# Down products of a feed-forward by seven products of quarters, and three of four weight sums by accumulating transfers

## The chip, the cores and the metric

The kernel runs on one core of one Trainium2 chip. The time is device microseconds from start to end of one execution. The kernel before took 2272.09 us in the median of 3 runs (2272.01 to 2272.13). The engines are named as the profile names them: PE multiplies matrices (PEld is its weight load), DVE, ACT and POOL work on vectors, SP issues transfers. Each engine works through its own queue in order; an instruction that waits holds up everything behind it on that engine.

## The reference

Two groups of tokens, 512 of a new stream and 32 of a running one, go through two layers of width 1024 and share all weights. Each layer is: half a feed-forward, a mixer (a Mamba-2 scan in layer 0, stick-breaking attention in layer 1), half a feed-forward, and a gated per-layer embedding (called PLE below). So there are four feed-forwards, and each computes

```python
def swiglu(h, w_gate, w_up, w_down):
    return (jax.nn.silu(h @ w_gate) * (h @ w_up)) @ w_down
x = x + 0.5 * swiglu(rms_norm(x, g), w_gate, w_up, w_down)   # 1024 -> 2816 -> 1024
```

Everything is in 32 bit floats. Between the second feed-forward and the third, keys and values for the attention are made from x.

## The kernel before, in words

The 544 tokens are the columns of every tile (two halves of 272), model and hidden width lie on the partitions in blocks of 128. The hidden width 2816 is 22 row blocks, the model width 8 chunks `x[0]` to `x[7]`. A product of a 128 x 128 weight block with 128 x 272 columns takes three matmuls, because every operand is split in a high part (`whi`, `xh`, `hh`: a rounding copy, made by ACT or POOL) and a low part (`wlo`, `xl`, `hl`: the difference, made by DVE or POOL): high by high, high by low, low by high. So one block on all 544 columns is 6 matmuls of 272 columns.

Class `Sevens` runs one feed-forward. Row blocks 0 to 3 of the hidden width are done plainly ("p" units: gate or up weights of one block, 48 matmuls). The other 18 go in 9 pairs. For a pair, gate and up weights are cut into quarters, and seven products of sums of quarters with sums of activation quarters (tiles `xfh`, `xfl`, made once per feed-forward) stand for eight. The seven are named by their weight operand: a11, s3 = a11+a21, s2 = s3+a22, a12, s1 = a21+a22, a22, s4 = s2+a12; each is a step of 24 matmuls. The four sums are made by DVE (a few by POOL). The results are put together, scaled by the norm's factor `r`, and turned into the hidden block. The down product is plain in the kernel before: for a group of 4 or 6 row blocks, eight "d" units, one per chunk m, with all blocks of the group accumulated in one bank of PSUM, then one DVE instruction (`leave`) that adds half of it to `x[m]`. The last group's d units stand at the end of the feed-forward; each `x[m]` that leaves them is at once prepared for the next norm (`Norm.ops`: xh by ACT, xl by DVE, a square by ACT, its sum into `acc` by POOL).

The order of all this is set by `Plan`: chains of work are generators that ask for slots, events and engines, and the planner, with fixed costs per instruction, lets the chain go next that can start first; where several could, the one with the lower rank goes (preparing the next norm 2, `leave` 9, weights 10, PE 20). What comes out is a fixed order of instructions on PE, DVE, ACT and POOL. The weights of a step may be split only into a free buffer of three (`NW = 3`): the buffer of the step three places earlier, which is free when PE has ended that step. Raw weights come by SP's queue into slots of their own, one for each quarter (`a11`, `a21`, `a22`, `a12`), which are refilled when they are free.

Nearly every instruction is recorded by one helper, so the profile gives all of them one line (L194) and tiles tell them apart. In the profile's names `mm` is a PSUM bank, `gu` a hidden block in work, `a` and `s` are raw quarters and their sums.

Of the kernel before, what the change touches and what calls it, by code (L numbers as in the profile page):

```python
# [49 lines left out]
FIRST = [0, 1, 2, 3], [0, 1, 2, 3], [0, 1, 2, 3], [0, 1, 2, 3]  # L50
GROUPS = [(4, 5), (6, 7)], [(8, 9), (10, 11)], [(12, 13), (14, 15)], [(16, 17), (18, 19), (20, 21)]
AFTER, UNTIL = 3, 14

NH = 6
# [127 lines left out]
def _body(tc, io):  # L182
# [22 lines left out]
    with ExitStack() as ctx:  # L205
# [17 lines left out]
        x = [pool.tile([P, T], F32, tag=f"x{c}", name=f"x{c}") for c in range(KC)]  # L223
# [209 lines left out]
        def opening(norm, psum, tmp):  # L433
# [8 lines left out]
            more = tmp.tile([P, 2, 512], F32, tag="a12", name="a12")[:, :, :].rearrange("p j k -> p (j k)")  # L442
# [112 lines left out]
        class Sevens:  # L555

            NW = 3

            def __init__(self, plan, i, norm, bank, tmp, ring, roles, after, first=(), opened=None, ahead=None, done=None):
                self.plan, self.i, self.bank, self.tmp, self.ring = plan, i, bank, tmp, ring
                self.groups, self.after, self.opened, self.norm, self.ahead, self.done = (FIRST[i],) + GROUPS, after, opened, norm, ahead, done
# [4 lines left out]
                self.hs, self.loaded, self.raw, self.gu = {}, {}, {}, {}  # L570
                self.units, waiting = [], []
                for g, items in enumerate(self.groups):
                    steps = sum(isinstance(it, tuple) for it in items) * 7
                    step = sent = 0
                    for it in items:
                        if not isinstance(it, tuple):
                            self.units += [("p", it, j) for j in range(2)] if it or not opened else []
                            continue

                        for s in (0, 3, 1, 2, 4, 5, 6) if g == 0 or not any(isinstance(v, tuple) for v in self.groups[0]) and it == items[0] and g == 1 else range(7):  # L580
                            self.units.append(("s", it, s))
                            step += 1
                            while waiting and step >= AFTER and sent < (step - AFTER + 1) * KC / (UNTIL - AFTER):
                                self.units.append(waiting.pop(0))
                                sent += 1
                    self.units += waiting
                    waiting = [("d", g, m) for m in range(KC)]
                self.units += waiting
                self.last_step = max(k for k, u in enumerate(self.units) if u[0] == "s")
# [4 lines left out]
            def members(self, g):  # L594
                return [f for it in self.groups[g] for f in (it if isinstance(it, tuple) else (it,))]


            def fetch_plain(self):
                i = self.i
                for k, u in enumerate(self.units):  # L600
# [7 lines left out]
                    if u[0] == "p":  # L608
                        self.raw[k] = fetch_w(io["wgu"][i, u[1], u[2]], 1024)
                    elif u[0] == "w":  # L610
                        self.raw[k] = fetch_w(u[1], 1024)
                    else:
                        fs = self.members(u[1])
                        self.raw[k] = fetch_w(io["wd"][i, u[2], :, fs[0] * P:(fs[-1] + 1) * P], len(fs) * P)
                    yield "spawn", self.arrive(("raw", k), 1.0 if k < 3 else 4.5)

            def fetch_quarter(self, name):
                r, c = int(name[1]) - 1, int(name[2]) - 1
                for items in self.groups:
                    for it in items:  # L620
                        if isinstance(it, tuple):
                            yield "get", name
                            t = self.raw[it, name] = self.tmp.tile([P, 2, 512], F32, tag=name, name=name)
                            nc.sync.dma_start(t, io["wgu"][self.i, it[r], :, :, c * 512:(c + 1) * 512].rearrange("j p k -> p j k"))
                            yield "spawn", self.arrive(("raw", it, name))
# [5 lines left out]
            def total(self, out, a, b):  # L631
                return either(self.plan, v_cost(1024), 2.4, lambda e: e.tensor_tensor(out=out, in0=a, in1=b, op=ALU.add))

            def weights(self):
                raw, tmp = self.raw, self.tmp
                for k, u in enumerate(self.units):
# [6 lines left out]
                    if u[0] != "s":  # L643
                        yield "wait", ("raw", k)
                        if u[0] == "d":
                            n = len(self.members(u[1])) * P
                        src, free = raw[k], "a12" if k == 0 and self.opened else "raw"
                    else:
                        it = u[1]
                        name = STEPS[u[2]][0]  # L650
                        if name[0] == "a":
                            yield "wait", ("raw", it, name)
                            src = raw[it, name]
                            if name == "a22":
                                free = "a22"
                        elif name == "s3":
                            yield "wait", ("raw", it, "a21")
                            yield "get", "s3"
                            src = raw[it, "s3"] = tmp.tile([P, 2, 512], F32, tag="s3", name="s3")
                            yield self.total(src, raw[it, "a11"], raw[it, "a21"])  # L660
                            yield "wait", ("part", self.index[it, 0])
                            yield "put", "a11"
                        elif name == "s2":
                            yield "wait", ("raw", it, "a22")
                            yield "get", "s2"
                            src = raw[it, "s2"] = tmp.tile([P, 2, 512], F32, tag="s2", name="s2")
                            yield self.total(src, raw[it, "s3"], raw[it, "a22"])
                            yield "spawn", self.release(("part", self.index[it, 1]), "s3")
                        elif name == "s1":
                            src = raw[it, "a21"]  # L670
                            free = "a21"
                            yield self.total(src, src, raw[it, "a22"])
                        else:
                            src = raw[it, "s2"]
                            free = "s2"
                            yield "wait", ("part", self.index[it, 2])
                            yield self.total(src, src, raw[it, "a12"])
                            yield "spawn", self.release(("part", self.index[it, 3]), "a12")
                        src = src[:, :, :].rearrange("p j k -> p (j k)")
# [11 lines left out]
                    yield "spawn", self.halve(k, n, src, hi, lo, free), -2 if k == 0 and self.opened else 10  # L691

# [12 lines left out]
            def dense(self):  # L705
                banks = {}
                for k, u in enumerate(self.units):
# [3 lines left out]
                    if u[0] == "s":  # L711
                        it, s = u[1], u[2]
                        name, place, slot = STEPS[s]
                        if s == 0:
                            A, B, D, X = self.roles
                            at = {"A": A, "B": B, "D": D}
                            self.roles = [B, A, D, X]
# [5 lines left out]
                        if s == 2:  # L723
                            yield "wait", ("c0", it)
                        elif s == 4:
                            yield "wait", ("c1", it)
                        elif s == 5:
                            yield "wait", ("c3", it)
                        elif s == 6:
                            yield "wait", ("c2", it)  # L730
                        yield "wait", ("part", k)
                        for c in range(4):
                            if isinstance(slot, int):
                                yield "wait", ("xf", c, slot)
                            yield "T", 0.753, lambda: self.step(ps, self.loaded[k], c, slot, s in (0, 1, 3) and c == 0, s in (3, 5, 6) and c == 3)
                        yield "put", "w"
                        if s in (0, 1, 2, 4):
                            yield "spawn", self.save(it, ps, {0: 0, 1: 3, 2: 1, 4: 2}[s]), 20
# [30 lines left out]
                    else:  # L769
                        g, m = u[1], u[2]  # L770
                        fs = self.members(g)
                        final = g == len(self.groups) - 1
                        b = self.roles[(0, 3, 2, 1)[(k - self.last_step - 1) % 4] if k > self.last_step else 3]
                        yield "wait", ("part", k)
                        yield "get", f"b{b}"
                        ps = banks[g, m] = self.bank(b)

                        early = len(fs) - 2 if final and m < 2 else len(fs)
                        order = [(k, ps, e) for e in range(early)]
                        if final and m == 1:  # L780
# [10 lines left out]
                        if m == KC - 1:  # L791
                            for _ in fs:
                                yield "put", "h"
# [1371 lines left out]
```

## Time and profile before

| | before |
|---|---|
| median of 3 runs | 2272.09 us |
| the profiled execution, first to last instruction | 2270.6 us |
| PE busy | 2245.7 us, 17937 matmuls |
| DVE, ACT, POOL busy | 1675.8, 1008.2, 575.8 us |
| granted TensorE clock, mean | 0.997 |
| HBM read | 204.83 MB, mean 93 GB/s with the writes |

Busy times can overlap on one engine: an instruction's record ends after the next has begun. The distance from one start to the next tells what an instruction costs in a dense stretch. The four feed-forwards lie at about 0 to 372, 810 to 1175, 1262 to 1633 and 1800 to 2171 us of the execution; the mixers lie between the first and second and between the third and fourth.

### The profile page before, as it was taken

To read this page: it belongs to the slowest core of one execution; us is meant where nothing else is said; L and a number is where in the kernel's file an instruction comes from. 1 tells how busy PE (TensorE), PEld (TensorE's weight loads), DVE (VectorE), ACT (ScalarE), POOL (GpSimd) and SP (SyncE) were. 2 spreads that over 40 slices of the span, in tenths; PEclk is the share of its full clock that TensorE was granted. 3 is DMA by queue.
4 is the path that set the end of the run, shared out by engine and by line. 5 is a ranking of instruction groups with operands and counts; after the bars stand their busy time and mean duration, and the time that the engine had idled before them with its cause. 6 is when DMAs were issued, how large, how long until landed. Compare 5 with 4: busy or idle time off the path is not lost.

```text
span 2270.6 us, 42781 instructions
## 1 busy us (share of the span) xinstructions
PE 2245.7 (99%) x17937; PEld 2200.5 (97%) x17937; DVE 1675.8 (74%) x2195; ACT 1008.2 (44%) x1478; POOL 575.8 (25%) x546
## 2 busy tenths in 40 slices
PE   9999999999999999999999999999999999999997
PEld 9999999999899999999999999999997999999997
DVE  7777786778877676777857767778689676777857
ACT  5333334567756453333345533333568343333353
POOL 1222222254323122221221121212244222222214
PEclk9999999999999999999999999999999999999998
DMA  5233323333333232333232423332311233233232
GB/s 169 85 96 105 97 66 89 113 110 96 114 101 96 86 119 85 93 107 95 65 108 85 132 80 107 93 104 69 88 49 52 61 112 99 83 108 94 68 101 77
DMA packets 111537, 213.18 MB, mean 94 GB/s; under 512 B 12401, under 2 KB 33521, under 8 KB 111345
## 3 DMA queue, kind: packets, MB, share of 16 engines
q1 hardware_dynamic: 108464, 204.92, 30.2%
q10 hardware_dynamic: 2880, 5.53, 0.7%
q8 instruction: 141, 2.31, 0.4%
q14 instruction: 52, 0.42, 0.1%
HBM read 204.83 MB, written 5.60 MB: 93 GB/s over the span
## 4 chain that ended last, share of the span: by engine, by line
PE 94%; DVE 3%; ACT 2%; issue 1%; DMA 1%; POOL 0%; SPq 0%; DVEq 0%; ACTq 0%; POOLq 0%
PE mm L194 83%; PE z L194 4%; PE aux L194 3%; PE f L194 1%; PE tr L194 1%; PE o L194 1%; DVE wlo L194 1%; ACT whi L194 1%; DVE x L194 0%; DVE fu L194 0%; DMA wraw<-in_wpg 0%; DVE xl L194 0%; DMA x<-in_x 0%; DVE rm L194 0%; DVE y L194 0%
## 5 line engine op out<-in xcount | busy, mean ns | idle before, releaser
L194 PE MATMUL mm<-xh,whi 128*128 128x272 f32 x2096 | 512.9, 293 | 2.0 <-ACT xh L194 0.6
L194 PE MATMUL mm<-xl,whi 128*128 128x272 f32 x2096 | 506.5, 289 | 0.3 <-DVE xl L194 0.3
L194 PE MATMUL mm<-xh,wlo 128*128 128x272 f32 x2096 | 504.9, 289 | 1.8 <-DVE wlo L194 1.8
L194 PEld LDWEIGHTS mm<-xh,whi 128*128 128x128 f32 x2096 | 356.9, 189 | 12.7 <-issue 9.2
L194 PEld LDWEIGHTS mm<-xh,wlo 128*128 128x128 f32 x2096 | 356.8, 189 | 2.2 <-DVE wlo L194 2.2
L194 PEld LDWEIGHTS mm<-xl,whi 128*128 128x128 f32 x2096 | 357.0, 189 | 0.5 <-DVE xl L194 0.5
L194 ACT ACTIVATE whi<-wraw 128x1024 fp32r<-128x1024 f32 (+3 forms) x217 | 186.3, 859 | 357.5 <-PE mm L194 258.3
L194 PE MATMUL mm<-xfh,whi 128*128 128x272 f32 x1152 | 332.4, 289 | 0.0
L194 PE MATMUL mm<-xfl,whi 128*128 128x272 f32 x1152 | 332.3, 288 | 0.0
L194 PE MATMUL mm<-xfh,wlo 128*128 128x272 f32 x1152 | 332.2, 288 | 0.0
L194 DVE TENSOR_TENSOR wlo<-wraw,whi 128x1024 fp32r<-128x1024 f32 (+3 forms) x252 | 255.7, 1015 | 69.5 <-ACT whi L194 53.1
L194 PE MATMUL mm<-hh,whi 128*128 128x272 f32 x1408 | 291.6, 288 | 0.0
L194 PE MATMUL mm<-hh,wlo 128*128 128x272 f32 x1408 | 291.2, 288 | 0.0
L194 PE MATMUL mm<-hl,whi 128*128 128x272 f32 x1408 | 291.0, 288 | 0.0
L194 ACT ACTIVATE whi<-a 128x1024 fp32r<-128x1024 f32 x127 | 134.8, 1062 | 320.4 <-PE mm L194 214.8
L194 DVE TENSOR_TENSOR wlo<-a,whi 128x1024 fp32r<-128x1024 f32 x145 | 178.0, 1227 | 102.2 <-ACT whi L194 67.7
L194 PEld LDWEIGHTS mm<-hl,whi 128*128 128x128 f32 x1408 | 221.4, 189 | 0.0
L194 PEld LDWEIGHTS mm<-hh,whi 128*128 128x128 f32 x1408 | 221.1, 188 | 0.0
L194 PEld LDWEIGHTS mm<-hh,wlo 128*128 128x128 f32 x1408 | 220.6, 189 | 0.0
L194 PEld LDWEIGHTS mm<-xfh,wlo 128*128 128x128 f32 x1152 | 217.1, 188 | 0.0
L194 PEld LDWEIGHTS mm<-xfl,whi 128*128 128x128 f32 x1152 | 217.1, 188 | 0.0
L194 PEld LDWEIGHTS mm<-xfh,whi 128*128 128x128 f32 x1152 | 217.0, 188 | 0.0
(296 smaller groups left out, 4077.6 us busy)
## 6 DMA issues: line engine op xcount, KB each, us to landing
a<-in_wgu SPq DMA_DIRECT2D x145, 512.0 KB, 3.9
wraw<-in_wd SPq DMA_DIRECT2D x128, 256.0 KB, 2.7
wraw<-in_win SPq DMA_DIRECT2D x41, 512.0 KB, 3.6
wraw<-in_wgu SPq DMA_DIRECT2D x29, 512.0 KB, 3.6
wraw<-in_wd SPq DMA_DIRECT2D x32, 384.0 KB, 3.2
ab<-acs_d SPq DMA_DIRECT2D x16, 512.0 KB, 4.6
wraw<-in_wout SPq DMA_DIRECT2D x16, 512.0 KB, 3.7
wraw<-in_wpg SPq DMA_DIRECT2D x16, 512.0 KB, 3.6
```

The source lines that it names most:

```text
L194: ins = getattr(self.engine, op)(*args, **kw)
```

## The change

The first 16 of the 18 paired row blocks now go through the down product by seven products of quarters too. Their hidden pairs are joined in groups of three, three and two (`UNITED`), and each group takes two units "h" (a = 0 and 1), each of seven steps; a step has 6 matmuls for each pair of the group, thus 18, 18 or 12. I write h(g,a), and x(p) for the gate and up steps of pair p. Step order in an h unit is a11, a12, s2, s3, s1, a22, s4. h(0,0) and h(0,1) follow x(3), h(1,0) and h(1,1) follow x(6), h(2,0) and h(2,1) follow x(8), the last. The other six row blocks stay plain: 0 to 3 in four units after x(0), 20 and 21 in two units at the very end (four chunks each, 12 matmuls a chunk).

The hidden activations need sums of quarters as well (`outcome`: four DVE instructions a pair, and seven quarters instead of four are split in high and low). A product of quarters is added straight to x from PSUM by DVE (`add`), up to the place where the bank is used on: the steps s2, s1 and s4 accumulate on top of a11's bank, and each may start only when the add of the step before on that bank has been done (the `saved` events).

Of the four weight sums, s3, s1 and, for gate and up, s4 are now made by transfers: a plain one of one quarter by SP, then an accumulating one of the other quarter, issued from POOL's queue (`added`, `fourth`). s2 stays on DVE or POOL, and so does s4 in the h units. Smaller parts: x lies in tiles of two chunks; raw weights in memory are laid out by quarter; and keys and values wait in DRAM between the two middle feed-forwards and come back by three transfers from POOL when the attention starts.

```diff
+NPLAIN = 4
+NPAIRS = 9
+UNITED = (0, 1, 2), (3, 4, 5), (6, 7)
...
+                for p in range(NPAIRS):
+                    self.loads.append(("x", p))
+                    self.units += [("s", ("x", p), s) for s in ((0, 3, 2, 1, 4, 5, 6) if p == 0 else range(7))]
+                    if p == 0:
+                        self.units += [("d", 0, q) for q in range(4)]
+                    for g, ps in enumerate(UNITED):
+                        if p == ps[-1] + 1:
+                            self.loads += [("h", g, a) for a in range(2)]
+                            self.units += [("s", ("h", g, a), s) for a in range(2) for s in (0, 3, 2, 1, 4, 5, 6)]
+                self.units += [("d", 1, q) for q in range(2)]
...
+            def added(self, key, tag, name):
+                yield "sleep", 4.5
+                yield "D", 1.0, lambda: G.dma_start(self.raw[key, tag][:, :self.width(key)], self.quarter_of(key, name), accum_op=ALU.add)
+                yield "sleep", 5.0
+                yield "set", ("raw", key, tag)
...
+            def fourth(self, it):
+                yield "wait", ("part", self.index[it, 2])
+                yield "D", 1.0, lambda: G.dma_start(self.raw[it, "s2"], self.quarter_of(it, "12"), accum_op=ALU.add)
+                yield "sleep", 5.0
+                yield "set", ("raw", it, "s4")
...
+                        if s in (2, 4, 5, 6):
+                            yield "wait", ("saved", it, {2: 0, 4: 2, 5: 1, 6: 4}[s])
                         yield "wait", ("part", k)
...
+            def add(self, it, s, ps, slot):
+
+                row, col = {0: (0, 0), 1: (1, 1), 2: (1, 0), 3: (0, 0), 4: (1, 1), 5: (1, 0), 6: (0, 1)}[s]
+                to = x2[2 * row + it[2]][:, :, col * H:(col + 1) * H]
+                yield "W", v_cost(T) + 0.06, lambda: V.scalar_tensor_tensor(out=to, in0=ps[:, :, :H], scalar=-0.5 if row else 0.5, in1=to, op0=ALU.mult, op1=ALU.add)
+                if slot:
+                    yield "put", slot
+                yield "set", ("saved", it, s)
...
-                for name in ("a11", "a21", "a22", "a12"):
-                    plan.add(9, self.fetch_quarter(name))
+                for tag, name, more in (("a11", "11", None), ("s3", "11", "21"), ("a22", "22", None), ("a12", "12", None), ("s1", "21", "22")):
+                    plan.add(9, self.fetch_quarter(tag, name, more))
```

Three places in the new order matter for what follows. The first is the end of the first feed-forward on DVE, before. `x5` to `x7` leave, `wlo_4279` is the low part of the first weights of the scan that comes next (PE's first instructions there are two high-part products of chunk 0, then one with this tile).

```order
L194 SCALAR_TENSOR_TENSOR x5_70<-mm_4180,x5_70 128x544
L194 TENSOR_TENSOR wlo_4230<-wraw_4117,whi_4229 128x768
L194 SCALAR_TENSOR_TENSOR xl5_4240<-x5_70,gains_64,xh5_4239 128x544
L194 SCALAR_TENSOR_TENSOR x6_71<-mm_4231,x6_71 128x544
L194 TENSOR_TENSOR wlo_4279<-wraw_4207,whi_4278 128x1024
L194 SCALAR_TENSOR_TENSOR xl6_4289<-x6_71,gains_64,xh6_4288 128x544
L194 SCALAR_TENSOR_TENSOR x7_72<-mm_4280,x7_72 128x544
L194 SCALAR_TENSOR_TENSOR xl7_4329<-x7_72,gains_64,xh7_4328 128x544
L194 TENSOR_TENSOR acc_4036<-acc_4036,sq_4332 128x544
```

The same end now, on DVE; chunks 6 and 7 are both in tile x3, and the scan's first low part is `wlo_4267`.

```order
L193 SCALAR_TENSOR_TENSOR x3_68<-mm_4307,x3_68 128x544
L193 SCALAR_TENSOR_TENSOR x3_68<-mm_4326,x3_68 128x544
L193 SCALAR_TENSOR_TENSOR xl5_4336<-x2_67,gains_64,xh5_4335 128x544
L193 SCALAR_TENSOR_TENSOR xl6_4346<-x3_68,gains_64,xh6_4345 128x544
L193 SCALAR_TENSOR_TENSOR xl7_4352<-x3_68,gains_64,xh7_4351 128x544
L193 TENSOR_TENSOR acc_4244<-acc_4244,sq_4361 128x544
L193 TENSOR_TENSOR wlo_4267<-wraw_4189,whi_4266 128x1024
```

The scan's first low part has moved from ahead of the last two chunks to behind the last sum of squares. On POOL the additions of squares that this last sum needs stand one behind the other; at the end of the third feed-forward (the attention comes next) two of the three transfers of keys and values stand between them.

```order
L193 TENSOR_TENSOR acc_18739<-acc_18739,sq_18819 128x544
L1559 DMA kt_18873<-kd_9468 128x1088
L1560 DMA vt_18874<-vd_9469 128x1024
L193 TENSOR_TENSOR acc_18739<-acc_18739,sq_18851 128x544
L1561 DMA vt_18874<-wd_9470 32x256
L193 TENSOR_TENSOR acc_18739<-acc_18739,sq_18853 128x544
```

The second square counted from the end (`sq_18853`, chunk 6) is the last that POOL adds; DVE adds the last itself. The third place is the unit h(2,0) of the first feed-forward on DVE: `mm_3927` is the bank of a11, s2, s1 and s4, `wlo_3988` and `wlo_4011` are the low parts for the steps a22 and s4, `gu` and `h4l` belong to the last pair's hidden blocks.

```order
L193 TENSOR_TENSOR gu1_3891<-gu1_3891 128x544
L193 TENSOR_TENSOR gu0_3864<-mm_3674,r_360 128x2x272
L193 SCALAR_TENSOR_TENSOR x0_65<-mm_3927,x0_65 128x2x272
L193 TENSOR_TENSOR wlo_3946<-s3_3681,whi_3945 128x512
L193 TENSOR_TENSOR gu0_3864<-gu0_3864 128x544
L193 TENSOR_TENSOR wlo_3965<-s1_3780,whi_3964 128x512
L193 TENSOR_TENSOR s2_3895<-s2_3895,a12_3742 128x512
L193 SCALAR_TENSOR_TENSOR x0_65<-mm_3947,x0_65 128x2x272
L193 TENSOR_TENSOR wlo_3988<-a22_3817,whi_3987 128x512
L193 TENSOR_TENSOR h4l_3985<-gu0_3864,h4h_3984 128x544
L193 TENSOR_TENSOR wlo_4011<-s2_3895,whi_4010 128x512
L193 SCALAR_TENSOR_TENSOR x2_67<-mm_3927,x2_67 128x2x272
```

The first row on x0 is the add after a11, the last row the add after s2; between the two stands the low part of s4's weights, which is three steps further on. In h(0,0) it is the low part of a22's weights that stands ahead of the add after s2, and in h(0,1), h(1,0) and h(1,1) no later weights do. The other three feed-forwards have the same order at these places.

More of the change, by code (lines that the diff above doesn't have):

```diff
@@ L569, in __init__ @@
                 self.forms = Forms(norm)
[L570 to L589, printed above, removed]
+                self.hs, self.hf, self.loaded, self.raw, self.gu = {}, {}, {}, {}, {}
+                self.units, self.loads = [], []
+                for f in range(NPLAIN):
+                    self.units += [("p", f, j) for j in range(2)] if f or not opened else []
+                for p in range(NPAIRS):
[8 more added lines that the diff above has]
+                self.units += [("d", 1, q) for q in range(2)]
+                self.last_step = max(k for k, u in enumerate(self.units) if u[0] == "s" and u[1][0] == "x")
                 if ahead is not None:
@@ L652, in weights @@
+                        if name in ("a11", "a12", "a22", "s3", "s1"):
                             yield "wait", ("raw", it, name)
                             src = raw[it, name]
[L654 to L662, printed above, removed]
+                            if name != "s3" and (name != "a12" or it[0] == "x"):
+                                free = name
@@ L668, in weights @@
+                            yield self.total(src[:, :n], raw[it, "s3"][:, :n], raw[it, "a22"][:, :n], n)
                             yield "spawn", self.release(("part", self.index[it, 1]), "s3")
[L669 to L672, printed above, removed]
[L673 to L678 removed]
```

295 lines of the change are left out of this document (183 added, 112 removed).

## The prediction

> **What bounds the kernel now.** I read the busy times first, then the chain of waits over the third feed-forward (1262 to 1633 us), then the busy times of a stretch inside the second one (columns: PE, PEld, DVE, ACT, POOL, granted clock, DMA share, GB/s), and last what PE waits for.
>
> ```profile
> span 2270.6 us, 42781 instructions
> PE 2245.7 (99%) x17937; PEld 2200.5 (97%) x17937; DVE 1675.8 (74%) x2195; ACT 1008.2 (44%) x1478; POOL 575.8 (25%) x546
> ...
> 1289.97 343.13 PE mm L194 x2733
> ...
> 880.00:1120.00 240.00, 240.00 (x1916) 240.00 (x1915) 180.68 (x205) 81.22 (x108) 50.16 (x44) 1.00 0.32 95
> ...
> PE mm L194 <- DVE wlo L194: 1.8, 2, 1.1
> PE mm L194 <- DVE sq L194: 1.7, 1, 1.7
> ```
>
> PE sets the end. Its chain runs through a whole feed-forward without a gap, at 343.13/2733 = 0.1256 us a matmul and the full clock. DVE is the next engine, busy 75% of the stretch (180.68 of 240), but nothing waits for it there; PE's longest waits for DVE's low parts and squares are 1.1 and 1.7 us in the whole execution. So two things count: how many matmuls go, and where the new order makes PE wait.
>
> **The saving.** A group of row blocks in h units is seven products of quarters for eight. Per feed-forward the down matmuls go from 22 x 8 x 6 = 1056 to 864 - 24 for 16 blocks: 16 x 48 = 768, times 7/8 = 672, plus 6 x 48 = 288 for the plain blocks, 960 in all. The orders agree: 384 fewer on PE, 96 in each feed-forward; gate and up stay as they were. 384 x 0.1256 = **48.2 us**, if PE stays without gaps.
>
> **Does DVE become the bound?** Rows of groups by tile and shape (last: busy us, mean ns | idle before):
>
> ```profile
> L194 DVE TENSOR_TENSOR s<-s,a 128x1024 f32<-128x1024 f32 x72 | 100.2, 1392 | 0.0
> L194 DVE TENSOR_TENSOR s<-a,a 128x1024 f32<-128x1024 f32 x36 | 45.2, 1254 | 0.0
> L194 DVE TENSOR_TENSOR a<-a,a 128x1024 f32<-128x1024 f32 x36 | 46.0, 1279 | 0.0
> L194 DVE SCALAR_TENSOR_TENSOR x<-mm,x 128x544 f32<-128x544 f32 x160 | 115.0, 719 | 85.5 <-PE mm L194 85.5
> L194 DVE SCALAR_TENSOR_TENSOR gu<-gu,gu 128x272 f32<-128x272 f32 x32 | 17.3, 541 | 0.2
> L194 DVE TENSOR_TENSOR wlo<-wraw,whi 128x1024 fp32r<-128x1024 f32 x125 | 159.6, 1277 | 48.7 <-ACT whi L194 42.9 <-POOL whi L194 4.7
> L194 DVE TENSOR_TENSOR wlo<-wraw,whi 128x512 fp32r<-128x512 f32 x93 | 64.9, 698 | 20.8 <-POOL whi L194 10.6 <-ACT whi L194 10.2
> L194 DVE TENSOR_TENSOR wlo<-wraw,whi 128x768 fp32r<-128x768 f32 x32 | 30.4, 951 | 0.0
> L194 POOL TENSOR_TENSOR wlo<-wraw,whi 128x512 fp32r<-128x512 f32 x38 | 54.4, 1431 | 96.7 <-ACT whi L194 54.6 <-DVE a L194 39.0 <-DMA wraw<-in_wd 3.1
> ```
>
> The change halves the group s<-s,a and drops the two below it: 36 x 1.39 + 36 x 1.25 + 36 x 1.28 = 141 us less. Added: 72 adds into x (0.72, 52 us), some 64,600 more columns of low parts (1.28 us per 1024 columns by 951/768 and 698/512 and above: 80 to 88 us), 32 sums of 768 and 4 of 512 (0.95 and 0.70: 33 us), 128 instructions of 272 columns for hidden sums (0.54: 69 us) and 64 hidden low parts (about 30 us). The sum is +124 us, 31 per feed-forward of about 360: DVE goes from 75% to about 86%. It stays under PE on average; it costs only where a wait of PE stands behind a queue. POOL gets 12 sums of 512 (1.43 each) and 163 issues of transfers; even at a us each that is 8% of the span on top of its 25%. ACT gets 110 copies of about 0.65 us on top of 44%. Neither comes near.
>
> **Waits inside h units.** a11, s2, s1 and s4 share one PSUM bank, so each of these steps waits for the add of the one before. What stands ahead of that add on DVE decides. Consecutive starts on DVE show the true spacing, and one row the delay from ACT's copy to DVE; the last three rows are ACT's copies.
>
> ```profile
> 1409.04 0.68 DVE L194 TENSOR_TENSOR wlo<-wraw,whi 128x512 fp32r<-128x512 f32 x1
> 1409.64 0.71 DVE L194 TENSOR_TENSOR hl<-gu,hh 128x544 fp32r<-128x544 f32 x1
> ...
> 359.39 0.96 DVE L194 TENSOR_TENSOR wlo<-wraw,whi 128x768 fp32r<-128x768 f32 x1
> 360.27 0.78 DVE L194 SCALAR_TENSOR_TENSOR xl<-x,gains,xh 128x544 fp32r<-128x544 f32 x1
> ...
> 1417.07 1.22 DVE L194 TENSOR_TENSOR wlo<-s,whi 128x1024 fp32r<-128x1024 f32 x1 [0.17 <-ACT whi L194]
> ...
> L194 ACT ACTIVATE whi<-wraw 128x512 fp32r<-128x512 f32 x86 | 54.4, 633 | 152.0 <-PE mm L194 118.6 <-DVE wlo L194 32.0 <-issue 1.4
> L194 ACT ACTIVATE whi<-wraw 128x768 fp32r<-128x768 f32 x24 | 20.3, 844 | 47.4 <-PE mm L194 36.0 <-DVE gu L194 9.2 <-issue 2.2
> L194 ACT ACTIVATE whi<-wraw 128x1024 fp32r<-128x1024 f32 x105 | 110.9, 1057 | 157.9 <-PE mm L194 103.7 <-issue 24.4 <-PE z L194 10.6
> ```
>
> In h(2,0) the steps run a11, a12, s2, s3, s1. The add after s2 stands behind the low part of s4's weights, whose buffer is free only when PE has ended s3, the step just before s1. So s1 starts late by 0.2 (PE to ACT) + 0.63 (copy of 512) + 0.17 + 0.60 (low part) + 0.72 (add) + 0.17 = 2.5 us (2.0 to 2.8), and all that PE has behind it waits too. The add after a11 stands there behind two hidden instructions of the last pair: 0.7 more (0 to 1.2). In h(0,0) the same add stands behind the low part of a22's weights, freed one step earlier, at the end of s2: 0.2 + 0.84 + 0.17 + 0.88 + 0.72 + 0.17 = 2.98, less the 18 matmuls of s3 that run meanwhile (2.26) = 0.7 (0.3 to 1). h(2,1) follows h(2,0) so closely that its accumulated sums are the tightest: 0.4 (0 to 2). Together 4.3 per feed-forward, **17.2 us** in four.
>
> **Waits at the ends of feed-forwards.** Rows around the end of the third one; PE's last two down matmuls are the first row.
>
> ```profile
> 1632.68 0.41 PE L194 MATMUL mm<-hh,wlo 128*128 128x272 f32 x2
> 1633.14 0.72 DVE L194 SCALAR_TENSOR_TENSOR x<-mm,x 128x544 f32<-128x544 f32 x1 [1.74 <-PE mm L194]
> 1633.90 0.75 ACT L194 ACTIVATE xh<-x,gains 128x544 fp32r<-128x544 f32 x1 [3.21 <-DVE x L194]
> 1634.55 0.65 ACT L194 ACTIVATE sq<-x 128x544 f32<-128x544 f32 x1
> 1635.10 0.61 ACT L194 ACTIVATE kk<-kv 64x512 fp32r<-64x512 f32 x1
> 1635.65 0.72 DVE L194 TENSOR_TENSOR acc<-acc,sq 128x544 f32<-128x544 f32 x1 [0.19 <-issue]
> 1636.69 1.23 DVE L194 TENSOR_TENSOR wlo<-wraw,whi 128x1024 fp32r<-128x1024 f32 x1 [0.32 <-ACT whi L194]
> 1626.32 1.37 POOL L194 TENSOR_TENSOR acc<-acc,sq 128x544 f32<-128x544 f32 x1 [3.16 <-ACT sq L194]
> 1630.83 1.79 POOL L194 TENSOR_TENSOR acc<-acc,sq 128x544 f32<-128x544 f32 x1 [3.14 <-DVE wlo L194]
> ...
> 1172.37 0.33 SPq L269 DMA_DIRECT2D wraw<-in_wpg  x1
> ```
>
> Now the scan's first low part stands behind the last sum of squares. From PE's end: x[7] leaves 0.2 to 0.9, ACT's xh of it at 0.96, then the squares of chunks 5, 6, 7 at 1.6, 2.2, 2.7 (spacings 0.65 and 0.55). POOL adds chunk 5 from 2.35 and chunk 6 until 5.1 (1.37 each), DVE adds chunk 7 from 5.2, the low part runs 5.9 to 7.1, PE goes on at 7.3. PE has four high-part matmuls ahead (0.5 us): **6.8 us** lost (6.0 to 7.5). Before the attention two DMA issues stand between POOL's additions; SP's issue takes 0.33 us, POOL's may take as little, or about as long as a POOL addition: 0.7 to 2.7 for both. I take 1.5, nearer to SP's row, and PE has only 0.25 us ahead: **8.5** (6.2 to 11.5). Before the two PLEs only the second weights' low part stands behind the sum: needed at 6.0, there at 7.3, 1.3 each (0 to 2.5). Together **17.9 us**. Keys and values through DRAM: kt is issued some 4 us after PE's end and takes a plain transfer's 3.9 us (row below), ACT's and DVE's copies of it stand behind the norm's factor, which by then is hardly ready: 1 (0 to 4, one transfer in full).
>
> [...]
>
> **The accumulating transfers.** No run here shows one. Plain ones:
>
> ```profile
> q1 hardware_dynamic: 108464, 204.92, 30.2%
> ...
> a<-in_wgu SPq DMA_DIRECT2D x145, 512.0 KB, 3.9
> wraw<-in_wd SPq DMA_DIRECT2D x128, 256.0 KB, 2.7
> ```
>
> One may land as fast as a plain one (3.9 us for 512 KB) or cost twice that, as if read and written back (7.8; 5.4 for 256 KB). In a pair s4's is the tightest: s2 is split, and its place free, 2.6 us into a pair of 7 x 3.01; s4 starts at 18.1, less copy, delay and low part (1.06 + 0.17 + 1.23) is 15.6, so 13 us are free. s3 of the pair after an h unit is tighter: its slot is free 4.4 us into the unit (15.8 us long), the plain load ends at 8.3, the step starts at 18.8, so 8 us are free. Tightest is s3 of h(2,1): its slot is free 4.2 us into h(2,0), plus 2.7 of load, plus the accumulation, plus 3.4 for s2's sum on POOL (1.43), copy, low part and delays, against 16.9 where s2 starts: 6.6 us for 256 KB. So even the double price fits, just, and I take no cost beyond the 0.4 above, for issues that stand behind POOL's other work. For the engines: 30.2% of 2270.6 us moved 204.92 MB, so 0.299 MB per us; a pair moves 8 quarters, 4.19 MB, 14.0 of 20.9 us, or 19.3 if accumulating counts twice: 67 to 92%.
>
> [...]
>
> **The sum.** -48.2 + 17.2 + 17.9 + 1 = -12.1, so a span of 2258.5. The median lies 1.5 above the span (2272.09 against 2270.6): **2260**. With every term at its low bound (h units 9.2, ends 12, DRAM 0) it is 2245; with all high (28, 24, 4) 2280.
>
> **Rivals.**
> - The whole saving: the next step's PE queue absorbs the adds, because DVE is 14% idle and reaches the low parts early. It speaks for it that PE waited for no add in 160 before; against it that those adds never stood ahead of a step on their own bank. 2272 - 48 = 2224.
> - Accumulating transfers land late (the slower side). One mechanism: issue to landing takes longer than the 8 us that s3 has after an h unit (8 places) and 6.6 in h(2,1) (4 places), since all 156 come from POOL's queue, behind its sums, and share engines that would be 67 to 92% busy. Each us beyond costs PE about a us at each place: from 9.5 us on it eats the gain (8 x 1.5), at 11 us for 512 KB and 8 for 256 it is 8 x 3 + 4 x 1.4 = 30: about 2290; beyond 13 the 36 sums s4 would follow, 36 per us. Against it: the 3.9 us row.
> - The losses are as large as the saving: h units and ends at their upper bounds and another 8 us, where DVE at 86% falls behind in h(·,1). About 2270.
> That the change doesn't remove matmuls is excluded by the counts.
>
> **How the numbers follow.** Forecast (2250 to 2268) 0.62, whole saving 0.09, late transfers 0.16, no gain left 0.13. A difference of 0.2% (4.5 us) is about what a measurement of this kernel can tell. Faster holds the first two: 0.71, rounded to 0.70; the same 0.13; slower 0.17. The range 2245 to 2282 takes the bounds of the unknown terms and the milder half of the late transfers.
>
> **What would show it.** 384 fewer matmuls; PE waiting about 2.5 us for DVE's x four times in h(2,0); two waits of 6 to 9 us for a low part, after the first and third feed-forward; DVE near 86% inside a feed-forward; sums from in_wgu landing under 8 us from POOL's issue; DMA share at 0.6 to 0.9 in pairs. PE waiting for whi or wlo made from s, many times, would be the late transfers and make the prediction wrong; so would a PE without waits in the h units.

## The result: 1% slower

| | before | changed |
|---|---|---|
| median | 2272.11 us (2272.01 to 2274.98, 4 runs) | 2295.72 us (2294.41 to 2297.62, 4 runs) |
| ratio | | 1.0102 [1.0088, 1.0116] |
| profiled span | 2270.6 us | 2292.6 us |

The forecast was 2260, the range ended at 2282. One execution of e7_chunks_early, listed below, took 12255 us and is left out of its ratio. The page of the changed kernel, busy times and queues:

```profile
span 2292.6 us, 42927 instructions
PE 2221.1 (97%) x17553; PEld 2166.0 (94%) x17553; DVE 1813.0 (79%) x2454; ACT 1095.1 (48%) x1588; POOL 687.3 (30%) x672
...
q1 hardware_dynamic: 92912, 232.19, 31.1%
q0 software_dynamic: 23120, 75.64, 18.6%
```

The matmuls did go: 17937 - 17553 = 384. But PE's busy time fell by 24.6 us, not 48.2, so part of the loss lies inside its busy time; and PE, idle for 24.9 us of the span before, is idle for 71.5 now. Both halves have to be found. What PE waits for (us in total, times, longest us):

```profile
PE mm L193 <- DVE x L193: 21.0, 16, 2.9
PE mm L193 <- DVE wlo L193: 14.6, 14, 7.9
PE z L193 <- DVE wlo L193: 9.0, 1, 9.0
```

And where, in the timeline of PE: h(0,0), the pair after h(0,1), h(2,0) twice and h(2,1) of the first feed-forward, its end, the end of the second (`plh`) and of the third:

```profile
176.48 0.36 PE L193 MATMUL mm<-h4h,whi 128*128 128x272 f32 x1 [0.73 <-DVE x L193]
203.31 0.39 PE L193 MATMUL mm<-xfh,wlo 128*128 128x272 f32 x1 [0.73 <-DVE wlo L193]
342.19 0.36 PE L193 MATMUL mm<-h4h,whi 128*128 128x272 f32 x1 [0.58 <-ACT gu L193]
347.74 0.37 PE L193 MATMUL mm<-h4h,whi 128*128 128x272 f32 x1 [2.27 <-DVE x L193]
360.61 0.36 PE L193 MATMUL mm<-h4h,whi 128*128 128x272 f32 x1 [0.57 <-DVE x L193]
385.79 0.82 PE L193 MATMUL mm<-xh,wlo 128*128 128x272 f32 x2 [7.91 <-DVE wlo L193]
...
1180.38 0.52 PE L193 MATMUL mm<-plh,whi 128*128 128x272 f32 x2 [2.86 <-DVE x L193]
...
1645.65 0.59 PE L193 MATMUL z<-xh,wlo 128*128 128x272 f32 x1 [8.99 <-DVE wlo L193]
```

The waits that were worked out beforehand stand where they were forecast, and most of them nearly as long. The 2.86 us at the end of the second feed-forward had been put at 1.3, and the wait in the pair after h(0,1) at nothing. What was not forecast at all shows in the busy times by stretch (columns: PE, PEld, DVE, ACT, POOL, clock, DMA share, GB/s):

```profile
348.00:352.00 4.00, 4.00 (x22) 4.00 (x22) 2.56 (x4) 0.63 (x1) 1.23 (x2) 0.57 0.78 139
2182.00:2186.00 4.00, 4.00 (x33) 4.00 (x34) 3.13 (x6) 1.26 (x2) 2.23 (x2) 1.00 0.88 158
1180.00:1184.00 4.00, 3.56 (x16) 3.16 (x17) 4.00 (x5) 2.48 (x4) 2.44 (x2) 0.66 0.20 52
384.00:388.00 4.00, 2.21 (x9) 2.21 (x10) 2.88 (x3) 0.00 (x0) 0.00 (x0) 0.50 0.29 61
388.00:392.00 4.00, 4.00 (x25) 3.84 (x25) 0.00 (x0) 0.54 (x1) 0.00 (x0) 0.83 0.59 201
```

PE is busy in all of the first stretch, but got 22 matmuls done instead of 33: after the stop of 2.27 us at 347.7 the clock was half for some 3.4 us. After the stop of 2.3 us in the fourth feed-forward (second row) it was not. It was half after both stops of 2.9 us before the embedding and both long ones. Why after one stop and not after another as long is worked out in the last section.

Here is the account, summed from the start of each matmul of 272 columns to that of the next, less 0.1255 us each: stops with a recorded wait; gaps about as long as the matmul itself; the rest of the gaps. A stop costs 0.16 us more than the wait that the profile shows (43 of 46 stops). The gaps of a matmul's length hold the half clock, but short gaps of other kinds as well. Before, the trace grants half clock to none of these matmuls but at the very end, so the 12.5 are nearly all of the other kinds. In the changed kernel 85 of them start in six stretches of half clock and lose 9.3 us there.

| kernel | span | stops | gaps of one matmul | rest | sum |
|---|---|---|---|---|---|
| before | 2270.6 | 10.5 | 12.5 | 8.2 | 31.2 |
| changed | 2292.6 | 61.5 | 24.0 | 11.4 | 96.9 |

That is 65.7 us more, less 48.2 saved: 17.5 of the 22.0 us by which the span grew. The other 4.5 lie in the attention, whose matmuls have other shapes; its part from the first low part to the next feed-forward is longer by 7.1 us in all (188.6 before, 195.7 now), with half clock in it too: 10.2 us of it behind the stop for `e`, where there were 3.4 before.

### The profile page after: what moved, and what is told of

Same layout as the page of the kernel before. It is cut to its first block, busy times and chain, and to the rows that moved or that the text cites. A ratio compares the mean times of both kernels' runs of the same rounds, so it can differ in the third digit from the quotient of the medians.

```text
span 2292.6 us, 42927 instructions
## 1 busy us (share of the span) xinstructions
PE 2221.1 (97%) x17553; PEld 2166.0 (94%) x17553; DVE 1813.0 (79%) x2454; ACT 1095.1 (48%) x1588; POOL 687.3 (30%) x672
## 3 DMA queue, kind: packets, MB, share of 16 engines
q1 hardware_dynamic: 92912, 232.19, 31.1%
q0 software_dynamic: 23120, 75.64, 18.6%
## 5 line engine op out<-in xcount | busy, mean ns | idle before, releaser
L193 ACT ACTIVATE whi<-s 128x1024 fp32r<-128x1024 f32 (+2 forms) x188 | 176.3, 938 | 399.6 <-PE mm L193 304.5
L193 DVE TENSOR_TENSOR wlo<-s,whi 128x1024 fp32r<-128x1024 f32 (+2 forms) x236 | 270.8, 1150 | 50.5 <-ACT whi L193 29.2
L193 ACT ACTIVATE whi<-a 128x1024 fp32r<-128x1024 f32 (+2 forms) x157 | 153.7, 979 | 252.7 <-PE mm L193 184.4
L193 PE MATMUL mm<-h4h,whi 128*128 128x272 f32 x896 | 229.8, 291 | 16.8 <-DVE x L193 14.6
L193 DVE TENSOR_TENSOR wlo<-wraw,whi 128x1024 fp32r<-128x1024 f32 (+2 forms) x154 | 191.3, 1244 | 64.1 <-ACT whi L193 51.8
L193 DVE TENSOR_TENSOR wlo<-a,whi 128x1024 fp32r<-128x1024 f32 (+2 forms) x181 | 197.3, 1090 | 43.8 <-ACT whi L193 41.4
L193 PE MATMUL mm<-h4h,wlo 128*128 128x272 f32 x896 | 228.5, 290 | 0.5 <-DVE wlo L193 0.5
L193 PE MATMUL mm<-h4l,whi 128*128 128x272 f32 x896 | 228.2, 290 | 0.0
L193 DVE SCALAR_TENSOR_TENSOR x<-mm,x 128x544 f32<-128x544 f32 x232 | 165.9, 721 | 63.5 <-PE mm L193 62.2
L193 ACT ACTIVATE whi<-wraw 128x1024 fp32r<-128x1024 f32 (+2 forms) x125 | 129.4, 1037 | 179.4 <-PE mm L193 98.8
```

The costliest lines, as they stand in the source:

```text
L193: ins = getattr(self.engine, op)(*args, **kw)
```

## Experiments

Theory O: the fixed order is at fault; work stands on DVE ahead of what PE needs. Theory T: sums made by accumulating transfers land late. Rival V: DVE is too full, so that no order helps. Theory C: a stop also costs half clock behind it. The account above, for each run:

| run | median us | ratio to before | span | stops | gaps of one matmul |
|---|---|---|---|---|---|
| changed | 2295.7 | 1.0102 [1.0088, 1.0116] | 2292.6 | 61.5 | 24.0 |
| e1_tail | 2291.1 | 1.0085 [1.0070, 1.0100] | 2288.4 | 55.6 | 24.4 |
| e2_adds | 2305.7 | 1.0146 [1.0129, 1.0163] | 2304.8 | 65.3 | 30.9 |
| e3l_all | 2295.8 | 1.0102 [1.0087, 1.0117] | 2291.6 | 55.0 | 26.8 |
| e4_idle_work | 2293.2 | 1.0092 [1.0077, 1.0107] | 2289.2 | 45.6 | 22.5 |
| e5_a12_first | 2280.9 | 1.0034 [1.0021, 1.0047] | 2276.7 | 49.4 | 22.8 |
| e6_half_accum | 2279.7 | 1.0036 [1.0023, 1.0049] | 2276.5 | 49.5 | 20.3 |
| e7_chunks_early | 2299.8 | 1.0117 [1.0097, 1.0137] | 2296.5 | 64.0 | 29.1 |
| e8_all | 2311.9 | 1.0168 [1.0145, 1.0190] | 2315.2 | 70.0 | 35.9 |
| e9_best | 2267.7 | 0.9976 [0.9964, 0.9989] | 2267.4 | 41.1 | 19.5 |
| e10_ends | 2282.3 | 1.0039 [1.0024, 1.0054] | 2281.3 | 52.5 | 19.6 |
| e11_s4_dve | 2322.5 | 1.0214 [1.0197, 1.0231] | 2326.8 | 83.4 | 34.5 |

**The low part ahead at the ends (e1_tail).**

```diff
-yield "spawn", self.halve(k, n, src, hi, lo, free), -2 if k == 0 and self.opened else 10
+yield "spawn", self.halve(k, n, src, hi, lo, free), -2 if k == 0 and self.opened else 1 if u[0] == "w" else 10
```

> Only the rank of the last weight split of the first and third feed-forward changes, so that its low part stands ahead of the next norm's work on DVE. If the fixed order on DVE is the cause (theory O), the waits of 7.9 and 9.0 us for that low part end, and the half clock that follows each of them (about 1.6 to 2 us each): -19 to -21 us, about 2275. If DVE is simply too full at a feed-forward's end (rival V), PE stops instead for the chunks' low parts that are now later on DVE, and less than 6 us are gained: above 2289. If late accumulating transfers are the cause (rival T), all the stops inside the feed-forwards stay and these two waits go: about 2279, without the clock.

Measured 2291.1 (the span is 4.2 us shorter; by the times alone the intervals overlap). The wait for the low part is gone, and PE waits 3 us of matmuls later instead (at the third end 6), for the sum of squares (timeline of PE):

```profile
386.68 2.15 PE L193 MATMUL aux<-acc,ones 128*128 128x272 f32 x4 [5.43 <-DVE acc L193]
...
1646.35 1.16 PE L193 MATMUL tr<-acc,ones 128*128 128x272 f32 x4 [2.02 <-DVE acc L193]
```

So the wait for the low part had hidden another one. Why the sum is late shows at the same end of the changed kernel, on DVE and on POOL:

```profile
378.32 4.33 DVE L193 SCALAR_TENSOR_TENSOR xl<-x,gains,xh 128x544 fp32r<-128x544 f32 x3 [0.17 <-ACT xh L193]
383.88 0.73 DVE L193 TENSOR_TENSOR acc<-acc,sq 128x544 f32<-128x544 f32 x1 [1.23 <-POOL acc L193]
...
375.12 8.72 POOL L193 TENSOR_TENSOR acc<-acc,sq 128x544 f32<-128x544 f32 x5 [1.53 <-ACT sq L193]
```

POOL needs 8.72/5 = 1.74 us for a chunk's addition, and DVE 4.33/3 = 1.44 for an `xl` that takes 0.78 alone, as both run at once (of these three the first took 0.79, the two that began inside an addition on POOL 1.86 and 1.85). A chunk leaves PE every 1.5 us here, since the last plain group has only two row blocks. Rival V's number held (above 2289), though PE waits for POOL's additions more than for the low parts that V had named: order alone moves the wait.

**The adds ahead (e2_adds).**

```diff
-yield "spawn", self.add(it, s, ps, f"b{b}" if s in (3, 5, 6) else None), 20
+yield "spawn", self.add(it, s, ps, f"b{b}" if s in (3, 5, 6) else None), 1
```

> Only the rank of the adds from PSUM to x changes, so that they go ahead of later weights' low parts on DVE. Theory O: the stops of 2.45 us in h(2,0), 0.9 us in h(0,0) and 0.7 us in h(2,1), four of each, end (16 us), and the two half-clock stretches after the stops in the first and third feed-forward (1.7 us each): -16 to -20 us, about 2277. Rival V (DVE too full): the stops come back as waits for low parts, less than 5 us gained. Rival T: the stops at s3 of the pair after an h unit are the larger ones and stay: no more than 8 us gained.

Measured 2305.7, 10 us slower than the changed kernel. All waits for x in the h units are gone. In their place PE waits for copies of sums (what PE waits for in this run):

```profile
PE mm L193 <- POOL whi L193: 12.0, 8, 2.5
PE mm L193 <- ACT whi L193: 6.0, 4, 2.1
```

One of them in PE's timeline:

```profile
303.42 0.59 PE L193 MATMUL mm<-xfh,whi 128*128 128x272 f32 x1 [2.51 <-POOL whi L193]
304.85 0.60 PE L193 MATMUL mm<-xfh,wlo 128*128 128x272 f32 x1 [0.60 <-DVE wlo L193]
```

These are the 8 places after an h unit and the 4 in h(2,1) that the prediction's second rival named. That one traced back, in the timelines of SP (the plain load) and POOL (the accumulating issue, the copy):

```profile
287.75 1.20 SPq L615 DMA_DIRECT2D s<-in_wgq  x2
...
291.57 0.89 POOL L193 DMA_DIRECT2D s<-in_wgq  x1 [5.12 <-DVE wlo L193]
...
301.34 2.03 POOL L193 TENSOR_SCALAR whi<-s 128x1024 fp32r<-128x1024 f32 x1 [3.64 <-DMA s<-in_wgq]
```

From POOL's issue to the copy that waited for it are 9.8 us. My expectation for T ("the larger ones stay") had the mechanism and not its size: with the stops of the h units gone, the sums had less time and took more than was gained. The account agrees: stops +3.8 us and gaps of one matmul, where the half clock lies, +6.9.

**More time for the sums (e5_a12_first), or half of their bytes (e6_half_accum).** Both start from the adds ahead. The first changes the order of steps in two pairs. The second leaves out half of the columns of every accumulated quarter (in `fourth` too, not shown).

```diff
-for s in ((0, 3, 2, 1, 4, 5, 6) if p == 0 else range(7))]
+for s in ((0, 3, 2, 1, 4, 5, 6) if p in (0, 4, 7) else range(7))]
```

> The adds ahead as in the run with the adds' rank (2305.7 us), and in the pairs that follow an h unit the step a12 comes second, so that s3 and s2, which need an accumulating transfer, come 3.0 us later. If PE there waited because the accumulating transfers land late (theory T), the waits for copies of s3 and the low parts behind them (12.0 + 7 us, with restarts) go at these 8 places and only those in h(2,1) stay: about 2286. If DVE is full (rival V), the same waits come back as waits for low parts: above 2300.

```diff
-G.dma_start(self.raw[key, tag][:, :self.width(key)], self.quarter_of(key, name), accum_op=ALU.add)
+G.dma_start(self.raw[key, tag][:, :self.width(key) // 2], self.quarter_of(key, name)[:, :self.width(key) // 2], accum_op=ALU.add)
```

> The adds ahead as above; the accumulating transfers add only the first half of each quarter's columns (the sums s3, s1 and s4 lack the other half), so they move half the bytes, with the same waits, issues and engine work. Theory T: the waits for copies of sums after h units and in h(2,1) go (18 us, with low parts and restarts some 27): about 2279. Rival V: no change but a little, above 2300.

Measured 2280.9 and 2279.7, 25 and 26 us less than 2305.7; T had said 2286 and 2279, V above 2300. The 12.0 us of waits for POOL's copies are gone from both. So late sums are shown as the cause of what the adds ahead brought out. DMA issues of the half run, then of the run with the adds ahead (KB each, median us to landing):

```profile
s<-in_wgq POOLq DMA_DIRECT2D x108, 256.0 KB, 4.9
```

```profile
s<-in_wgq POOLq DMA_DIRECT2D x108, 512.0 KB, 7.5
```

Half the bytes land 2.6 us earlier in the median, with nothing else changed.

**All ranks at once (e3l_all), the chunks earlier (e7_chunks_early), and all together (e8_all).**

> Both changes of rank, and the last chunks' leaving ahead of the next norm's work on DVE. Theory O: -20, -18, and at the two ends before the per-layer embedding the waits of 2.9 us for x with their half clock, 8 together: about 2250, faster than the kernel before. Rival V: the waits move, above 2280. Rival T: 2270 to 2280.

Measured 2295.8: with the adds and the low part ahead, and chunks leaving at rank 1 instead of 9, the waits at the ends before the embedding are gone, those for late sums and for the sum of squares are there. That is V's range (above 2280), with T's waits in it.

```diff
-                self.units += [("d", 1, q) for q in range(2)]
+                                if g == len(UNITED) - 1:
+                                    self.units.append(("d", 1, a))
```

> As the changed kernel, but of the last plain unit's eight chunks those four that h(2,1) doesn't touch (0, 1, 4, 5) come before h(2,1), so that only four chunks leave at the end. If PE's stops at the ends come from eight chunks leaving in 12 us, for each of which DVE, ACT and POOL need 1.3 to 1.75 us (theory O: order), they shrink from 7.9, 2.9, 9.0 and 2.9 to 2 at most, their half clock goes, and h(2,1) waits less: about 2268. If these engines are full anyway (rival V), the work is late elsewhere: above 2285.

Measured 2299.8: the long waits at the ends shrink to 2.0 and 3.7 us for the sum of squares (O had said 2 at most), but h(2,1) now begins with four stops of 2.7 us for a low part, since DVE makes the early chunks' `x` and `xl` there, and before the embedding PE still waits 2.9 us, now for its input's low part.

> All at once: chunks early, adds ahead, the next matrix's first low part ahead, a12 second in the pairs after an h unit. If the three causes (ends, adds behind low parts, sums that land late) are independent and complete: about 2250, faster than the kernel before. Rival V: above 2275.

Measured 2311.9, the second worst. Adding up gains went wrong: with h(2,0) free of stops, which the run before still had, the early chunks come before the last pair's hidden blocks are ready, and PE waits 3.1 us for them in each feed-forward, with half clock behind:

```profile
357.88 0.82 PE L194 MATMUL mm<-h4h,whi 128*128 128x272 f32 x2 [3.11 <-ACT h4h L194]
```

**Useless work in a stop (e4_idle_work).**

```diff
+for _ in range(30):
+    for a in range(2):
+        TE.matmul(sides(ps)[a], nones, v[:, a * H:(a + 1) * H], start=True, stop=True)
```

> 60 useless matmuls (7.5 us) fill most of PE's wait at the end of the first and the third feed-forward; the waits are there as before. If each of these stops costs more than its length, since the clock granted after it is half for some 3.4 us (theory C), 3 to 4 us are gained: about 2292. If the clock's row is only a record of the stop and costs nothing by itself: 2295.7, no change; if the useless work holds up later work: slower.

Measured 2293.2. By the times alone this can't be told from 2295.7 (the intervals overlap); the trace can. In the same stretch as above the clock is now full:

```profile
384.00:388.00 4.00, 3.80 (x28) 3.39 (x27) 3.00 (x3) 0.00 (x0) 0.09 (x1) 1.00 0.24 52
388.00:392.00 4.00, 4.00 (x31) 3.84 (x30) 0.07 (x1) 1.87 (x3) 0.00 (x0) 1.00 0.60 210
```

and the scan and the attention come earlier: the first wait in the scan by 1.3 us (564.76 to 563.42), and in all 3.3 us by the attention's longest stop (1732.93 to 1729.64). The span is 3.4 shorter, within the 3 to 4 of theory C, but in part by luck. From h(2,0) of the feed-forward to the next stage's first waits, the first end gains 1.5 us and the third 1.3: that much is the useless work. Elsewhere the second feed-forward lost 1.8 in longer waits for late sums and gained 0.8 at its end, and after the stop of 2.27 us in the third one the clock happened to stay full, 1.6 gained.

**Sums s4 on DVE again (e11_s4_dve).**

> As the changed kernel, but the 36 sums s4 of the pairs are made by DVE (or POOL) again instead of by an accumulating transfer; 72 of 108 accumulating transfers from the gate and up weights stay. Some 46 us of work come to DVE. If transfers hold PE up (theory T), s3 lands earlier after h units: up to 6 us faster, about 2290. If DVE's load holds it up (rival V): slower, above 2300. If neither is near its limit inside the pairs: 2295, no change.

Measured 2322.5, 27 us slower. With 46 us more of sums, DVE falls behind in the h units (what PE waits for):

```profile
PE mm L193 <- DVE x L193: 39.0, 23, 2.9
```

So the accumulating transfers earn more than they cost here: DVE has no room for what they took from it. V was right about DVE, T about the remaining late sums; they aren't exclusive.

**The ends with less work on POOL (e10_ends), and everything that held (e9_best).** Both add to the low part's rank that chunks leave with rank 1, that DVE does the last four additions of squares (three more than before, the last was its own already), and that SP issues the loads of keys and values; the second adds the adds ahead and a12 second.

```diff
-e, cost = (V, v_cost(T)) if c == KC - 1 else (G, 1.3)
+e, cost = (V, v_cost(T)) if c >= self.by_dve else (G, 1.3)
-nc.gpsimd.dma_start(kt, kept[0])
+nc.sync.dma_start(kt, kept[0])
```

> Only the ends of the feed-forwards change, as compared with the changed kernel: the next matrix's first low part and the leaving chunks go ahead of the next norm's work, the last four of the eight additions of squares go from POOL to DVE, and the three transfers of keys and values are issued by SP. The first run on the ends (2291.1 us) took only the low part ahead and left PE waiting 5.4 and 2.0 us for the sum of squares. If that sum, added on POOL at 1.75 us a chunk while a chunk leaves every 1.5 us, is what was left (theory O), all four stops shrink to 1 us or less and their half clock goes: 22 + 6 us, about 2268. If DVE has no room for the additions (rival V), chunks leave later and PE waits for x or xl: above 2285.

> The same ends together with the adds ahead and a12 second in the pairs after an h unit (2280.9 us by themselves). If ends, adds and late sums are separate causes: another 17 us of stops and some 4 us of half clock less, about 2260, and so 0.5% faster than the kernel before. If DVE can't take it (rival V): no better than 2278.

Measured 2282.3 and 2267.7: 13 us less than the changed kernel where 28 were expected, and 28 where 36 were. The first of them meets neither O's 2268 nor V's 2285. The second is faster than the kernel before, ratio 0.9976 [0.9964, 0.9989]. The end of the first feed-forward still has a wait of 4.4 us for the sum of squares (it was 5.4): DVE, with three more additions, is itself late.

```profile
385.17 2.15 PE L193 MATMUL aux<-acc,ones 128*128 128x272 f32 x4 [4.36 <-DVE acc L193]
```

## Why the prediction was wrong

The direction failed. The forecast span was 2258.5, the measured one is 34.1 us longer. Two steps failed in their reasoning: stops were priced by their length alone, with no term for the half clock behind them, and the accumulating transfers were put at no cost. The rest are terms that were too small, each worked out from the matmuls' starts:

| term | predicted | measured |
|---|---|---|
| saving, 384 matmuls | -48.2 | -48.2 |
| waits in h units | 17.2 | 20.4 |
| low parts of s3 and s2 in the pairs after them | 0 | 6.7 |
| first steps of pairs, waiting for ACT's copy `c` | 0 | 1.6 |
| ends | 17.9 | 23.3 |
| gaps of one matmul, 9.3 of them at half clock after stops | no term | 11.5 |
| attention, beyond its end | 1 | 4.5, half clock included |
| smaller gaps | no term | 3.2 |
| stops that both kernels have | no term | -1.0 |
| sum | -12.1 | 22.0 |

- **The saving** and **DVE's average load** were right: 384 matmuls, and DVE at 84% of the stretch that was shown of before (200.87 of 240), where 86% was forecast for a feed-forward. DMA is at 69%, within the 67 to 92%.

```profile
880.00:1120.00 240.00, 238.24 (x1891) 237.38 (x1890) 200.87 (x244) 98.67 (x127) 68.93 (x64) 1.00 0.69 178
```

- **Waits inside h units**: the add after s2 in h(2,0) cost 2.44 to 2.48 us in all four feed-forwards (2.5 forecast), that in h(0,0) 0.84 to 0.92 (0.7). The stop of 0.7 after a11 came, but the releaser shown is ACT's `gu`. h(2,1) had an add late as well, 0.73 instead of 0.4.
- **The accumulating transfers** are a step that failed in its reasoning. "So even the double price fits, just, and I take no cost beyond the 0.4 above" compared 8 us with 7.8. The median was 6.6 us for 512 KB, inside the bounds, but after an h unit it took 9.0 (from POOL's row in the timelines to ACT's):

```profile
s<-in_wgq POOLq DMA_DIRECT2D x108, 512.0 KB, 6.6
```

```profile
191.69 0.88 POOL L193 DMA_DIRECT2D s<-in_wgq  x1 [0.32 <-DVE x L193]
...
200.68 1.06 ACT L193 ACTIVATE whi<-s 128x1024 fp32r<-128x1024 f32 x1 [4.82 <-DMA s<-in_wgq]
202.04 1.22 DVE L193 TENSOR_TENSOR wlo<-s,whi 128x1024 fp32r<-128x1024 f32 x1
```

  A bound that just fits a median doesn't fit the places where transfers bunch. The h units' own stops gave the sums some of the time that they lacked: late sums show as 6.7 us here, and as 25 once the adds go ahead.
- **The ends**: the two long stops were 7.9 and 9.0 us (6.8 and 8.5 forecast), as POOL's additions took 1.74 us (the first end's mean; 1.35 to 1.83 at the third) and not 1.37; the other POOL row of before, 1.79 beside DVE's `xl`, was the nearer one. Before the embedding the stop was 2.9 and not 1.3, and not for the second low part: the embedding's first product waits for a chunk that is late in leaving its bank.
- **Half clock** has no term in the prediction at all, though the trace of before showed it, in the attention (PE's timeline, then the clock by stretch: 0.68):

```profile
1718.62 0.50 PE L194 MATMUL z<-kk,qq 128*128 128x512 f32 x1 [3.39 <-DVE e L194]
```

```profile
1720.00:1725.00 5.00, 4.54 (x24) 4.15 (x24) 5.00 (x8) 4.07 (x10) 3.05 (x3) 0.68 0.01 2
```

So a term could have been estimated from it: half clock lasted 3.41 us there, half of which is 1.7 for a stop, and with the six stops above 2 us that were forecast 10 us in all. That stops of 2.5 us are long enough for it no row of before shows, and only two of the four were; the other two of the six stretches follow the stops before the embedding.
- **The second rival** named the right places, and its time (2290) is near the measured one, but in the changed kernel itself it is a minor part. The first rival's ground, that PE would absorb the adds, is refuted by the adds' waits.

The attention's longer body is explained in part. From the stop for `e` to the next feed-forward it takes 103.2 us before and 108.4 now. In e5_a12_first, where half clock behind that stop lasted 3.4 us as before, it takes 105.8; so about 2.6 of the 5.3 are half clock. The rest stays open: the waits for `e` and `p` (2.9 us, and 2.0 or 1.6) are in every run, keys and values issued by SP or by POOL, and no run took them back to SBUF. Before, the wait for `e` was longer (3.39), that for `p` 0.46.

## What to carry to other kernels

When an engine is bound at 99% and the next at 75%, a saving on the first that adds work to the second is not priced by the second's average: follow each step's chain at the places where steps are short, and where stops of 2 us and more appear, allow for the half clock that can follow them (here six stretches, behind stops of 2.27 to 8.99 us, cost 9.3 us). Two late chains can hide each other, so that taking one stop away brings out another; a gain found by moving one thing ahead has to be measured with the other in place. A transfer's time has to be taken where transfers bunch (9.0 us here after an h unit), not as a median (6.6).

## What the runs showed of the hardware

- Stops of PE of only 2.27 us were followed by half clock at 348 and at 1606 us, of 2.31 and 2.32 us at 1148 and 2182 were not. The traces show why. In all 13 of them the stretches of half clock start on one grid of 3.413 us, with a place of its own in each execution, and last one step of it or several (in the changed kernel at 348.43 us and 10, 244, 369, 378, 406 and 547 steps later, for one to three steps, and after PE's last matmul); what they follow is how long PE idles inside one step. The stop at 348 lies in one step, that at 1148 across two (columns as above; idle is the length less PE's busy time):

```profile
345.01:348.43 3.42, 1.15 (x9) 0.95 (x8) 3.42 (x7) 1.18 (x2) 1.75 (x2) 1.00 0.82 237
348.43:351.84 3.41, 3.41 (x17) 3.41 (x16) 1.97 (x3) 0.63 (x1) 0.86 (x1) 0.50 0.84 146
...
1143.73:1147.14 3.41, 1.74 (x15) 1.52 (x13) 3.41 (x7) 1.47 (x3) 1.97 (x2) 1.00 0.73 233
1147.14:1150.56 3.42, 2.77 (x22) 2.81 (x23) 2.75 (x5) 0.63 (x1) 0.86 (x1) 1.00 0.97 187
```

  With 2.27 us idle in one step the next has half clock; with 1.67 and 0.65 none follows. The stops at 1606 and 2182 do the same (2.25 in one step; 1.84 and 0.47). Of the steps at full clock in the changed kernel, half clock followed all eight with 2.01 us idle or more and none with 1.84 or less; over the 13 traces it always followed more than 1.91, and never less than 1.23; between, both occur. So in e9_best a stop of 1.38 us cost clock (1.68 idle in its step with smaller gaps), and in e7_chunks_early two of 2.91, each split over two steps, did not.
- The queue of the accumulating transfers (q0) cost the DMA engines 18.6% of the span for 75.64 MB, SP's plain ones (q1) 31.1% for 232.19: 1.84 times as much for a byte. Landing took 6.6 us for 512 KB where SP's plain ones into the same tiles took 4.4, and the issue itself 0.88 us on POOL against 0.33 on SP.
